# A hybrid attention layer on one Trainium2 core: the first gate's loads and sums given out among the first attention units

## The chip, the cores and the metric

The kernel is one launch on one core of a Trainium2 chip. The metric is the device time in microseconds of that launch, as a median of several runs. The engines are named as in the profile: PE (TensorE, matmuls), PEld (its weight loads), DVE (VectorE), ACT (ScalarE), POOL (GpSimd) and SP (SyncE, which issues the DMAs here).

## The reference, cut to what matters

The layer works on 512 tokens of width 1024. A vector `c` is multiplied into six modulation vectors; the third of them, `gt1`, is the first gate, and it is used only after the attention's output projection.

```python
mod = c @ w_ada[l] + b_ada[l]
sh1, sc1, gt1, sh2, sc2, gt2 = jnp.split(mod, 6, axis=-1)
h = rms_norm(x, g_pre_mix[l]) * (1.0 + sc1[:, None]) + sh1[:, None]
proj = h @ w_in[l]
...
o_nsa = nsa_attention(...)   # compressed, selected and windowed branches, gated
o_dsa = dsa_attention(...)   # a top-k choice of keys from an index, then attention
o = jnp.concatenate([o_nsa, o_dsa], axis=-1) @ w_out[l]
x = x + gt1[:, None] * rms_norm(o, g_post_mix[l])
h = rms_norm(x, g_pre_ffn[l]) * (1.0 + sc2[:, None]) + sh2[:, None]
y = jnp.square(jax.nn.relu(h @ w_up[l])) @ w_down[l]
x = x + gt2[:, None] * rms_norm(y, g_post_ffn[l])
```

## The kernel before, in words

All matmuls that need precision are split: an operand is rounded on ACT (`L123`, "hi") and the rest is subtracted on DVE or POOL (`L124`, "lo"), and each product is three matmuls. The stages are:

- **First projection (about 20 to 82 us).** Modulation columns for the first norm, then the column chunks A and B of `w_in` for all four token tiles.
- **Chunks D, C and E (about 82 to 190 us).** `proj` (`L392`) makes 24 matmuls for each of four token tiles: `pj_D`, `pj_C`, `pj_E`. Beside them run the rotary products (`rope`, `L398`, on DVE and POOL), the stacking and transposing of heads (`stack`, `stack_T`), the compressed keys and values (`cmp_pack`, `cmp_mm`: tiles `kcp_k`, `kcp_v`, `hid_k`, `hid_v`), the index scores of the top-k (`index_step`, `L549`: matmul `ix`, relu `rl` on ACT, weighted sum `wk` on DVE) and the top-k itself (`topk_round`, `L565`: sixteen rounds of MAX8 and MATCH_REPLACE8 on DVE for each of three token tiles).
- **Attention units (about 158 to 360 us).** Twelve units (`UNITS`, `L51`): a kind of attention ("s", "w" or "d") and a token tile. Each unit makes score matmuls `s_*`, a masked maximum on DVE (`L876`), an exponential on ACT (`L877`), scalings on DVE, transposes `tp_*`, and the product `O*`. The output projection (`op`, `L1006`) and the next norm are mixed in.
- **MLP (about 385 to 720 us).** Matmuls `up` and `dn`, back to back.

The order of the first 360 us is written by hand. `PLAN` (`L41`) is a table that gives each group of steps a start and a length in slots. `place` (`L813`) spreads the steps of a group evenly: step q of n goes to start + (q + 0.5) / n * length, and the integer part is its slot. Slots 0 to 18 are emptied one by one by the loop at `L832`, beside the steps of chunks D and C. Slots 19 to 34 are emptied by the loop over the units (`run(la, lc, slot(n + 19))`, near `L1090`), mixed with that unit's steps. The tile framework's scheduler then reorders each engine's instructions within what the program's dependences allow.

The group of the change is `g1`, the first gate (`g1_steps`, `L731`, over `vec_steps`, `L704`). It has 23 steps: one that loads the norm weights and two bias rows (`bb`, 256 KB each, broadcast to all partitions, in two of six buffers of a pool named `m2`); two loads of `wv_g` (512 KB each, in two buffers); six empty steps; then eight groups of four matmuls (`vs_g`, `L718`) that add up one half of the vector, each of the first six followed by the load of the next piece into the buffer just read. After the fourth and after the eighth group `finish` adds the bias on DVE (`L743`), spreads the row over the partitions with one matmul (`gv_g`, `L745`) and multiplies with the norm weights on DVE (`L746`). While it is being summed a half holds one PSUM bank of the tag "S", of which there are four; `pj_*`, `ix`, `s_*`, `op` and others use the same four. The result is first read by `outp_steps` (`L1012`) in slot 25. The same `vec_steps` makes `a2` (slots 25 to 27) and `sh2` (slots 29 to 32) later, from tiles `wv_a` and `wv_sh`, through the same two load buffers.

Of the kernel before, what the change touches and what calls it, by code (L numbers as in the profile page):

```python
# [45 lines left out]
    x22=(32.6, 0.1), h22=(33.35, 1.68), x23=(33.6, 0.1), sD=(0, 0.48), cl=(0.2, 4.48), lC=(0.5, 0.1),  # L46
    sC=(3.7, 2.94), lE=(8.2, 0.1), sE=(8.3, 5.379), ix=(8.2, 5.88), cpe=(10, 0.1), ck1=(11.1, 1.077),
    cv1=(13.2, 0.784), ck2=(11.7, 2.8), ck3=(15, 2.8), cv2=(14.6, 0.98), cv3=(15.2, 1.05), tk1=(13, 6),
    g1=(6, 8),
)  # L50
UNITS = [("s", 0), ("w", 0), ("s", 1), ("w", 1), ("d", 0), ("d", 1),  # L51
         ("s", 2), ("w", 2), ("d", 2), ("s", 3), ("w", 3), ("d", 3)]
# [1147 lines left out]
```

## Time and profile before

| what | value |
|---|---|
| runs | 733.19 us median of 3 (732.59 to 735.87) |
| the profiled execution's own time | 734.76 us |
| its span, first to last instruction | 733.0 us |
| mean granted clock of PE | 0.966 |
| busy: PE, DVE, ACT, POOL | 690.3, 457.1, 332.1, 129.2 us |

The profile names an instruction by its line, its engine, and what it writes and reads, with buffer numbers left out (`pj_C<-uh_C,hh`). A busy matmul row counts the time until its modelled end, and rows overlap; so the distance from one start to the next says more than the length of one. `x8` in a row of `vs_g` is one group of four matmuls (each makes two instructions). In brackets stands how long the engine had been idle, and what ended that.

### The profile page before, as it was taken

The page shows a single profiled execution, that of the slowest core. Times are in us where ns is not written, and L with a number is a line of the kernel's source. Part 1 is how long each engine was busy: PE and PEld are TensorE (multiplying, and loading weights), DVE is VectorE, ACT ScalarE, POOL GpSimd, SP SyncE. Part 2 cuts the span into 40 slices and gives each one's busy share as a digit, 9 for nine tenths or more (in the row PEclk, how much of TensorE's full clock was granted, in tenths as well). Part 3 has the DMA queues.
Part 4 walks back from the last instruction along what each step waited for, and adds up shares of the span by engine and source line. Part 5 has one row for each costly group of instructions (what it writes and reads, how often), then busy time and mean ns, then how long its engine had stood idle before and what let it go on. Part 6 is the DMA issues. An engine that isn't in the chain of part 4 may idle for free.

```text
span 733.0 us, 9979 instructions
## 1 busy us (share of the span) xinstructions
PE 690.3 (94%) x3601; PEld 539.3 (74%) x3601; DVE 457.1 (62%) x978; ACT 332.1 (45%) x691; POOL 129.2 (18%) x196
## 2 busy tenths in 40 slices
PE   4998979899989999899999999999999999999995
PEld 2776967788755576465699888888888888788884
DVE  4444637979989978774685464654734445443547
ACT  5433783725778569554475313322331332323222
POOL 3000193544634144222020000000000000000003
PEclk9999998969889999999999999999999999999998
DMA  8996451450006571462122352533415133231202
GB/s 246 312 322 211 115 172 59 110 120 1 1 1 161 172 185 30 115 230 86 58 87 66 103 164 99 170 117 116 132 64 178 58 114 115 81 121 58 86 1 114
DMA packets 67612, 87.15 MB, mean 119 GB/s; under 512 B 3974, under 2 KB 38890, under 8 KB 67563
## 3 DMA queue, kind: packets, MB, share of 16 engines
q1 hardware_dynamic: 67562, 86.52, 39.0%
q8 instruction: 28, 0.46, 0.3%
q14 instruction: 22, 0.17, 0.1%
HBM read 84.40 MB, written 2.10 MB: 118 GB/s over the span
## 4 chain that ended last, share of the span: by engine, by line
PE 77%; DVE 9%; DMA 7%; ACT 3%; issue 2%; SPq 2%; POOL 1%; POOLq 0%; DVEq 0%; ACTq 0%
PE up L1113 22%; PE dn L1154 22%; PE op L1006 6%; PE O L905 4%; PE pj_E L323 2%; PE pA L323 2%; DMA wm<-in_w_ada_dram 2%; PE pj_D L323 2%; PE pj_C L323 2%; PE pB L323 1%; SPq L161 1%; PE tp_w L899 1%; PE hid_v L622 1%; DVE m L567 1%; DMA rwA<-in_w_in_dram 1%
## 5 line engine op out<-in xcount | busy, mean ns | idle before, releaser
L1113 PE MATMUL up<-hh,uh_U 128*128 128x512 f32 (+1 forms) x288 | 104.6, 366 | 0.6 <-ACT hh L123 0.6
L1113 PE MATMUL up<-hh,ul_U 128*128 128x512 f32 (+1 forms) x288 | 104.9, 366 | 0.0
L1113 PE MATMUL up<-hl,uh_U 128*128 128x512 f32 (+1 forms) x288 | 104.0, 366 | 0.0
L1154 PE MATMUL dn<-uh_D,al 128*128 128x512 f32 x256 | 99.6, 389 | 0.0
L1154 PE MATMUL dn<-uh_D,ah 128*128 128x512 f32 x256 | 98.7, 391 | 0.0
L1154 PE MATMUL dn<-ul_D,ah 128*128 128x512 f32 x256 | 98.5, 389 | 0.0
L124 DVE TENSOR_TENSOR ul_D<-rw_D,uh_D 128x1024 fp32r<-128x1024 f32 (+1 forms) x35 | 41.3, 1181 | 47.7 <-ACT uh_D L123 45.4
L1160 DVE TENSOR_TENSOR y<-dn,y 128x512 f32<-128x512 f32 x56 | 38.3, 689 | 49.5 <-PE dn L1154 49.4
L206 POOL TENSOR_SCALAR ms<-sy 128x1 f32<-128x1 f32 x4 | 3.6, 912 | 341.6 <-ACT fj L1133 341.6
L1113 PEld LDWEIGHTS up<-hh,uh_U 128*128 128x128 f32 x288 | 54.3, 188 | 9.6 <-ACT hh L123 0.9
L1117 ACT ACTIVATE rl<-up 128x512 f32<-128x512 f32 x32 | 19.1, 598 | 92.6 <-PE dn L1154 59.2
L1113 PEld LDWEIGHTS up<-hh,ul_U 128*128 128x128 f32 x288 | 54.3, 189 | 8.8
L1113 PEld LDWEIGHTS up<-hl,uh_U 128*128 128x128 f32 x288 | 53.7, 189 | 9.0 <-DVE hl L124 0.2
L123 ACT CAST uh_U<-rw_U 128x1024 fp32r<-128x1024 f32 x32 | 33.7, 1052 | 55.1 <-PE dn L1154 51.9
L123 ACT CAST uh_D<-rw_D 128x1024 fp32r<-128x1024 f32 (+1 forms) x36 | 36.2, 1010 | 46.2 <-PE up L1113 37.5
L1154 PEld LDWEIGHTS dn<-uh_D,al 128*128 128x128 f32 x256 | 48.1, 188 | 10.2 <-issue 0.2
L1154 PEld LDWEIGHTS dn<-uh_D,ah 128*128 128x128 f32 x256 | 48.1, 188 | 10.1 <-issue 0.2
L1154 PEld LDWEIGHTS dn<-ul_D,ah 128*128 128x128 f32 x256 | 48.1, 188 | 10.1
L124 DVE TENSOR_TENSOR ul_U<-rw_U,uh_U 128x1024 fp32r<-128x1024 f32 x32 | 39.1, 1222 | 11.6 <-ACT uh_U L123 10.7
L1118 DVE TENSOR_TENSOR rl<-rl 128x512 f32<-128x512 f32 x32 | 22.1, 690 | 34.8 <-ACT rl L1117 34.8
L123 ACT CAST ah<-rl 128x512 fp32r<-128x512 f32 x32 | 19.8, 620 | 29.3 <-DVE rl L1118 29.2
L124 DVE TENSOR_TENSOR al<-rl,ah 128x512 fp32r<-128x512 f32 x32 | 22.0, 689 | 11.0 <-ACT ah L123 11.0
(407 smaller groups left out, 1486.2 us busy)
## 6 DMA issues: line engine op xcount, KB each, us to landing
rw_U<-in_w_up_dram SPq DMA_DIRECT2D x32, 512.0 KB, 4.7
rw_D<-in_w_down_dram SPq DMA_DIRECT2D x32, 512.0 KB, 3.6
wm<-in_w_ada_dram SPq DMA_DIRECT2D x32, 256.0 KB, 6.3
wv_g<-in_w_ada_dram SPq DMA_DIRECT2D x8, 512.0 KB, 6.2
rwo_a<-in_w_out_dram SPq DMA_DIRECT2D x16, 256.0 KB, 4.5
wv_a<-in_w_ada_dram SPq DMA_DIRECT2D x8, 512.0 KB, 5.5
rwo_b<-in_w_out_dram SPq DMA_DIRECT2D x16, 256.0 KB, 4.1
wv_sh<-in_w_ada_dram SPq DMA_DIRECT2D x8, 512.0 KB, 4.4
```

The source lines that it names most:

```text
L123: A.copy(hi, src)
L124: eng.tensor_tensor(lo, src, hi.bitcast(F32), op=OP.subtract)
L161: mod_in[k].append(SY.dma_start(wt[hf][:, v], wa[:, hf * 4:hf * 4 + 4, v * D + k * P:v * D + (k + 1) * P]))
L323: PE.matmul(ps[:, :n], l[:, t, k, :], r[:, k % 2, :n], start=(k == 0 and i == 0), stop=(k == KT - 1 and i == 2))
L567: mx = V.max(m8, work[t])
L905: mm = [PE.matmul(O[j][g * 64:(g + 1) * 64, :], vn[kb][:, self.vsl[g]:self.vsl[g] + 64], pts[kb, g][0], start=(first and kb == 0), stop=(l ...
L1006: PE.matmul(stt["ps"], l[:, kk, :], r[:, kk % 2, :], start=(kk == 0 and i == 0), stop=(kk == 7 and i == 2))
L1113: PE.matmul(pv[:, t0:t1, :], l[:, k % 2, fs], r[:, t0:t1, k, :], start=(n == 0), stop=(n == 23))
L1117: A.activation(rl, ps, AF.Relu)
L1118: V.tensor_tensor(rl, rl, rl, op=OP.mult)
L1154: PE.matmul(ps, l[:, t * P:(t + 1) * P], r[:, f % 2, :], start=(n == 0), stop=(n == 11))
L1160: V.tensor_tensor(ya, ps, ya, op=OP.add)
```

## The change

One pair of numbers in `PLAN`: the 23 steps of `g1` start at slot 17 and take 6 slots, where they started at slot 6 and took 8.

```diff
 PLAN = dict(
...
     cv1=(13.2, 0.784), ck2=(11.7, 2.8), ck3=(15, 2.8), cv2=(14.6, 0.98), cv3=(15.2, 1.05), tk1=(13, 6),
-    g1=(6, 8),
+    g1=(17, 6),
 )
```

By the formula the first sum moves from slot 9.3 to slot 19.5, and the last step from slot 13.8 to slot 22.9. What the scheduler makes of that is shown at three places.

**PE, from the last matmul of `pj_C` for token tile 0 to the first for tile 1.** `skp_ks` are transposes of keys, `kcT` is the transpose for the compressed keys, `ix_1_2` and `ix_1_3` are index scores. Before:

```order
L323 MATMUL pj_C_0_1140<-uh_C3_1021,hl_1_177 128x512
L417 MATMUL skp_ks3_1047<-identr_109,sk_ks3_969 128x128 x2
L417 MATMUL skp_ks0_1095<-identr_109,sk_ks0_1000 128x128 x2
L486 MATMUL kcT_1043<-ident_104,pjB_2_710 128x128
L552 MATMUL ix_1_2_1178<-k1a_685,qi_0_884 128x256
L553 MATMUL ix_1_2_1178<-k2a_686,qi_0_884 128x256
L718 MATMUL vs_g10_1173<-wv_g12_1184,c_sb_67 32x256 x4
L417 MATMUL skp_ks1_1167<-identr_109,sk_ks1_1040 128x128 x2
L718 MATMUL vs_g10_1173<-wv_g13_1259,c_sb_67 32x256 x4
L552 MATMUL ix_1_3_1186<-k1a_685,qi_0_884 128x256
L553 MATMUL ix_1_3_1186<-k2a_686,qi_0_884 128x256
L323 MATMUL pj_C_1_1210<-uh_C0_950,hh_1_176 128x512
```

And with the change:

```order
L323 MATMUL pj_C_0_1130<-uh_C3_1015,hl_1_177 128x512
L486 MATMUL kcT_1033<-ident_104,pjB_2_710 128x128
L417 MATMUL skp_ks3_1037<-identr_109,sk_ks3_969 128x128 x2
L417 MATMUL skp_ks0_1085<-identr_109,sk_ks0_1000 128x128 x2
L552 MATMUL ix_1_3_1169<-k1a_685,qi_0_884 128x256
L553 MATMUL ix_1_3_1169<-k2a_686,qi_0_884 128x256
L417 MATMUL skp_ks1_1157<-identr_109,sk_ks1_1030 128x128 x2
L323 MATMUL pj_C_1_1193<-uh_C0_950,hh_1_176 128x512
```

The third and fourth group of sums are gone from here (the first two stood a few rows earlier, inside `pj_C_0`), and `ix_1_2` has taken their place inside `pj_C_0`. In the built program `pj_C_1` has the PSUM bank that `ix_1_0` had, before and after; the relu that empties that bank is on ACT.

**PE, around the hidden layer of the compressed values (`hid_v`).** Before:

```order
L718 MATMUL vs_g11_1407<-wv_g16_1427,c_sb_67 32x256 x4
L622 MATMUL hid_v_1550<-kcp_v_1485,w1_v0_888 128x62 x8
L622 MATMUL hid_v_1550<-kcp_v_1485,w1_v1_890 128x62 x2
L417 MATMUL skp_C00_1581<-identr_109,sk_C00_1451 128x128 x2
L718 MATMUL vs_g11_1407<-wv_g17_1467,c_sb_67 32x256 x4
L417 MATMUL skp_C00_1581<-identr_109,sk_C00_1451 128x128 x2
L417 MATMUL skp_C01_1587<-identr_109,sk_C01_1454 128x128 x4
L622 MATMUL hid_v_1550<-kcp_v_1485,w1_v1_890 128x62 x6
L745 MATMUL gv_g11_1505<-bb_1_1019,ones_111 128x512
L552 MATMUL ix_3_3_1508<-k1a_685,qi_2_983 128x512
L553 MATMUL ix_3_3_1508<-k2a_686,qi_2_983 128x512
L323 MATMUL pj_E_0_1725<-uh_E0_1121,hh_1_176 128x512
```

With the change, eleven matmuls of `pj_E` for tile 0 stand ahead of `hid_v` (the last two of them are shown), and no sum of the gate is near:

```order
L323 MATMUL pj_E_0_1671<-uh_E1_1234,hh_1_176 128x512
L323 MATMUL pj_E_0_1671<-ul_E1_1235,hh_1_176 128x512
L622 MATMUL hid_v_1486<-kcp_v_1429,w1_v0_888 128x62 x8
L417 MATMUL skp_C00_1517<-identr_109,sk_C00_1401 128x128 x4
L417 MATMUL skp_C01_1523<-identr_109,sk_C01_1404 128x128 x4
L622 MATMUL hid_v_1486<-kcp_v_1429,w1_v1_890 128x62 x8
L323 MATMUL pj_E_0_1671<-uh_E1_1234,hl_1_177 128x512
```

**PE, between `pj_E` for tile 1 and for tile 2, with the change.** `s_s0_5` and `s_s0_6` are scores of the first attention unit. `wv_g10` and `wv_g11` are the two pieces that are loaded early; `wv_g12` is loaded into the buffer of `wv_g10`, whose group stands 17 rows above `wv_g12`'s:

```order
L323 MATMUL pj_E_1_1721<-uh_E3_1413,hl_1_177 128x512
L718 MATMUL vs_g10_1733<-wv_g11_1628,c_sb_67 32x256 x3
L873 MATMUL s_s0_5_1764<-k1s_687,qC_0_1516 128x128
L874 MATMUL s_s0_5_1764<-k2s_688,qC_0_1516 128x128
L718 MATMUL vs_g10_1733<-wv_g11_1628,c_sb_67 32x256
L873 MATMUL s_s0_6_1774<-k1s_687,qC_0_1516 128x128
L874 MATMUL s_s0_6_1774<-k2s_688,qC_0_1516 128x128
L417 MATMUL skp_C11_1578<-identr_109,sk_C11_1471 128x128 x4
L417 MATMUL skp_C20_1594<-identr_109,sk_C20_1510 128x128 x4
L718 MATMUL vs_g10_1733<-wv_g12_1769,c_sb_67 32x256 x4
L323 MATMUL pj_E_2_1797<-uh_E0_1111,hh_1_176 128x512
```

These sums are new here. The fourth group stands after `pj_E` for tile 2, the other four and both `gv_g` among the scores of the units "w" 0, "s" 1 and "w" 1.

On SP the norm weights and the first two pieces of `wv_g` stay where they were, in the first 45 us. The other six, and both loads of `bb`, move from the place after the loads of `rw_E` to a place after the first four pairs of `rwo_a` loads, one after the other, and directly ahead of the first two loads of `wv_a`.

## Rows read from the trace of the kernel before

**Rows 1.** The page: its first line and the busy time of each engine.

```profile
span 733.0 us, 9979 instructions
...
PE 690.3 (94%) x3601; PEld 539.3 (74%) x3601; DVE 457.1 (62%) x978; ACT 332.1 (45%) x691; POOL 129.2 (18%) x196
```

**Rows 2.** The table by windows from 100 to 240 us. Columns: the window, its length, busy us (and number) of PE, PEld, DVE, ACT and POOL, the granted clock of PE, the DMA engines' busy share, GB/s.

```profile
100.00:110.00 10.00, 6.07 (x48) 3.57 (x46) 1.55 (x4) 7.51 (x21) 9.10 (x18) 0.84 0.82 255
110.00:120.00 10.00, 9.19 (x39) 6.74 (x36) 6.04 (x17) 2.65 (x8) 1.91 (x5) 0.65 0.34 107
...
130.00:140.00 10.00, 10.00 (x66) 7.57 (x65) 10.00 (x25) 7.94 (x16) 6.37 (x8) 1.00 0.05 19
140.00:150.00 10.00, 8.09 (x54) 6.60 (x52) 8.49 (x20) 3.24 (x9) 3.69 (x5) 0.72 1.09 262
150.00:160.00 10.00, 10.00 (x40) 7.94 (x37) 7.17 (x19) 2.29 (x5) 3.83 (x6) 0.60 0.58 141
160.00:180.00 20.00, 19.23 (x113) 15.96 (x112) 19.28 (x72) 9.76 (x32) 10.12 (x15) 1.00 0.00 1
180.00:200.00 20.00, 18.97 (x112) 15.48 (x112) 19.53 (x76) 13.82 (x48) 12.94 (x22) 0.89 0.00 1
...
230.00:240.00 10.00, 8.56 (x72) 4.63 (x71) 10.00 (x28) 6.84 (x18) 4.10 (x4) 1.00 0.81 236
```

**Rows 3.** The chain that ended last, from 101 to 126 us. Columns: start, us, what.

```profile
102.45 6.48 DMA wv_g<-in_w_ada_dram
...
113.09 7.45 PE pj_C L323 x24
```

**Rows 4.** The timeline of PE from 101 to 113.5 us. Columns: start, length, engine, line, operation, what it writes and reads, count, and the idle time before it with what ended it.

```profile
101.75 1.07 PE L718 MATMUL vs_g<-wv_g,c_sb 128*32 128x256 f32 x16
...
105.35 0.33 PE L486 MATMUL kcT<-ident,pjB 128*128 128x128 f32 x1 [0.88 <-POOL pjB L406]
105.43 0.36 PE L552 MATMUL ix<-k1a,qi 128*128 128x256 f32 x1
...
108.97 1.08 PE L718 MATMUL vs_g<-wv_g,c_sb 128*32 128x256 f32 x8 [3.06 <-DMA wv_g<-in_w_ada_dram]
...
112.29 0.58 PE L552 MATMUL ix<-k1a,qi 128*128 128x256 f32 x1 [0.81 <-DVE bb L743]
...
112.89 0.63 PE L323 MATMUL pj_C<-uh_C,hh 128*128 128x512 f32 x1
```

**Rows 5.** The timeline of ACT from 104 to 116 us, same columns.

```profile
104.21 0.59 ACT L528 COPY pjC<-pj_C 128x512 f32<-128x512 f32 x1 [1.70 <-PE pj_C L323]
...
107.19 1.50 ACT L609 COPY kcp_k<-kcT 64x256 f32<-64x256 f32 x4
...
109.04 0.38 ACT L555 ACTIVATE rl<-ix 128x256 f32<-128x256 f32 x1
...
114.63 0.30 ACT L410 CAST sk_kw<-pjD 128x128 fp32r<-128x128 f32 x1 [0.84 <-DVE wk L559]
```

**Rows 6.** The timeline of POOL from 101 to 106 us, same columns.

```profile
101.52 2.38 POOL L124 TENSOR_TENSOR ul_E<-rw_E,uh_E 128x1024 fp32r<-128x1024 f32 x1
```

**Rows 7.** What DVE waited for between 100 and 222 us. Columns: DVE's instruction, what released it, us in total, times, longest.

```profile
DVE bb L743 <- PE vs_g L718: 7.9, 2, 6.1
...
DVE peT L600 <- PE pep_k L598: 2.4, 1, 2.4
DVE hx L629 <- PE hid_v L622: 1.9, 1, 1.9
...
DVE g L746 <- PE gv_g L745: 0.6, 1, 0.6
...
DVE wk L557 <- ACT rl L555: 0.4, 1, 0.4
```

**Rows 8.** The timeline of DVE, from 104 to 123 us and from 122 to 165 us: the first two bias sums, the first round of the top-k, the two gate products, the first masked maximum of the attention.

```profile
111.55 0.69 DVE L743 SCALAR_TENSOR_TENSOR bb<-bb,vs_g 128x512 f32<-128x512 f32 x1 [6.11 <-PE vs_g L718]
...
115.52 0.41 DVE L567 MAX8 m<-wk 128x8 f32<-128x256 f32 x1
...
129.17 0.67 DVE L746 TENSOR_TENSOR g<-gv_g,g 128x512 f32<-128x512 f32 x1
...
150.29 0.69 DVE L743 SCALAR_TENSOR_TENSOR bb<-bb,vs_g 128x512 f32<-128x512 f32 x1 [1.80 <-PE vs_g L718]
...
160.59 0.27 DVE L876 CUSTOM_DVE_ANT_0 P_s<-s_s,mask 128x128 f32<-128x128 f32 x1
```

**Rows 9.** The timeline of PE from 136 to 157 us.

```profile
136.54 0.64 PE L718 MATMUL vs_g<-wv_g,c_sb 128*32 128x256 f32 x8
137.11 0.50 PE L552 MATMUL ix<-k1a,qi 128*128 128x512 f32 x1
...
142.96 0.64 PE L718 MATMUL vs_g<-wv_g,c_sb 128*32 128x256 f32 x8 [1.06 <-DMA wv_g<-in_w_ada_dram]
144.45 4.53 PE L622 MATMUL hid_v<-kcp_v,w_v 128*128 128x62 f32 x20 [0.85 <-DVE kcp_v L612]
...
156.20 0.63 PE L323 MATMUL pj_E<-uh_E,hh 128*128 128x512 f32 x1
```

**Rows 10.** The view of the tile `wv_g`: from the issue of a load to its landing.

```profile
DMA to landing us min/median/max: 4.5/6.2/8.2
```

**Rows 11.** What PE waited for between 76 and 260 us: the sums of the later vector `a2`, by the same code.

```profile
PE vs_a L718 <- DMA wv_a<-in_w_ada_dram: 1.3, 1, 1.3
```

## Prediction

> **What bounds the kernel now.** I read the page first, then the table by windows, then the chain, and last the timelines of PE, ACT and DVE where the first gate stands. PE is busy for 690.3 of 733.0 us [rows 1], and the MLP, the last half, has no gaps; a change of order can win only before it. The table by windows shows where [rows 2]: from 100 to 110 us PE has 6.07 us of work and DVE 1.55; from 100 to 120 and from 140 to 160 us the granted clock is 0.60 to 0.84, so that part of the time PE works at 1.2 instead of 2.4 GHz. From 160 us on DVE is the fullest engine (19.28 and 19.53 of 20 us). The chain says what ends last in the first gap: a load of `wv_g` for 6.48 us and, behind the sums, the bias sum and an index score, the 24 matmuls of `pj_C` that take 7.45 us [rows 3]. The gate is not needed until slot 25, far later.
>
> So the two stretches are weighed apart from what follows. In the stretches (100 to 160 us) PE stalls and DVE stalls behind it. In the first attention units (160 to 220 us) DVE is full, and what arrives there is paid mostly in full. What counts is when DVE reaches the first masked maximum of the attention, at 160.59 us before [rows 8].
>
> **Part 1: the gap at 102 to 113 us.** Before, PE waits 3.06 us for the third piece and 0.81 us for the bank that the bias sum empties, and `pj_C` for tile 1 starts at 112.89 [rows 4]. With those sums gone it does not start at once: it needs the bank of `ix_1_0`, and the relu that frees it comes late in ACT's queue. Before, that relu ran from 109.04 to 109.42, behind the copy of `pj_C` (from 104.21), six key copies and four copies of `kcp_k` (1.50 us) [rows 5]. Now `pj_C_0` ends 0.8 us sooner (1.07 us of sums leave, one index pair comes, 0.3 us as an estimate from the 0.36 us of one `ix`, whose matmuls overlap [rows 4]), and two of the four copies stand behind the relu (0.75 us). `kcT`, which held PE until 105.35, does not hold it now: a 2.38 us subtraction on POOL has moved behind what `kcT` waits for [rows 4, 6]. So the relu ends at about 107.9 and `pj_C_1` starts 5.0 us earlier. PE still idles for some four of the five us before, so I let the low clock stand. If it stayed at 2.4 GHz, PE would gain at most the 0.35 that a mean of 0.65 leaves out [rows 2] of the 7.45 us of `pj_C` [rows 3], 2.6 us; DVE, which decides, gets none of it.
>
> DVE gains less than PE. Its first top-k round began at 115.52 [rows 8]. After the relu ACT has a second relu, the two copies of `kcp_k`, three key copies, a cast, two relus and a cast (0.38 + 0.75 + 1.1 + 0.3 + 0.8 + 0.3 = 3.6 us; copies and relus at the relu's 0.38 each, casts at 0.30 [rows 5]). Then come POOL's selection and what belongs to it, 0.9 us as from the last cast at 114.63 to the round at 115.52 [rows 5, 8]: 107.9 + 3.6 + 0.9 = 112.4. That is **3.1 us** (the bias sum's 0.69 us is inside). Two later waits of DVE go as well, for `peT` (2.4) and for a relu (0.4) [rows 7], since PE is five us early there and DVE three: **2.8 us**.
>
> **Part 2: 128 to 160 us.** Three more DVE instructions leave, 0.67 + 0.69 + about 0.68 us [rows 8]: **2.0 us**. Three waits leave: 1.8 us for the eighth group (the rest of the 7.9 us is part 1's 6.1), 1.9 for `hid_v`, 0.6 for the second spreading [rows 7]: **4.3 us**. `hid_v` was late because PE waited 1.06 us for the seventh piece and 0.85 us for `kcp_v`, and then did its 20 rows in 4.53 us at the low clock, until `pj_E` began at 156.20 [rows 2, 9]. Now eleven matmuls of `pj_E` cover the wait for `kcp_v`. I find PE some 5 us ahead of DVE at the first masked maximum, so DVE decides. Sum so far: 3.1 + 2.8 + 2.0 + 4.3 = **12.2 us**, DVE at about 148.4.
>
> **Part 3: what arrives at 150 to 205 us.** DVE gets its four instructions back: 0.69 + 0.69 + 0.67 + 0.68 = **2.7 us**, in full. PE gets eight groups and two spreadings. A group takes 0.57 us from start to start (136.54 to 137.11 [rows 9]), a spreading 0.50, as the index matmul of the same 128x512 in those rows: 4.6 + 1.0 = 5.6 us. PE has slack (19.23 and 18.97 of 20 us busy [rows 2], and the 5 us lead), but four PSUM banks limit how far it runs ahead, and one of them is now held by the sums. Between 0 and 5.6 I take **2.0 us**. The third piece can be loaded only when the first group has been read; a load takes 4.5 to 8.2 us to land [rows 10], and between the two groups stand some 3 us of PE work by the order. So PE waits 1.5 to 3 us there, and perhaps again at the seventh piece; less what DVE's own work covers I take **1.0 us** (bounds 0 and 6.1, twice the 3.06 of [rows 4]). Two of six `m2` buffers are held by `bb` here; two rotary products of `pj_E` now share one buffer, and a third takes `bb`'s first after the spreading: **0.5 us** (0 to 2). SP pays nothing: its queue is empty of other needs there (DMA share 0.00 to 0.01 [rows 2]), and the first loads of `wv_a`, now behind `wv_g`, still come some slots ahead of their use. The start of the kernel is unchanged, for the first two pieces stay there. After 220 us all waits are relative to what came before, so the lead is carried to the end.
>
> **Sum:** 12.2 - 2.7 - 2.0 - 1.0 - 0.5 = **6.0 us** less. The profiled execution took 734.76 us, so 728.8; it lies 1.6 us above the median of 733.19, and in terms of that median I predict **727.2 us**.
>
> One rule I weigh against this. Rows first: a wait for one piece (3.06 us, and 0.88 just before) was followed by a clock that fell from 1.00 to the low level and a mean of 0.65 over 110 to 120 us [rows 2, 4]; yet the same kind of sums for `a2`, which waited 1.3 us for a load, ran in a window with a clock of 1.00 [rows 2, 11]. The Trainium skill, "TensorE: Matmul & The Clock Gate", section "HAM oscillation — how this bites in real kernels", tells of a kernel whose short bursts of matmuls each wait for a DMA, and whose every burst then runs cold. By that rule the moved groups would bring the low clock along. The first case above agrees with it, the second does not.
>
> **Rivals.**
> - *The stall moves along (slower).* Six pieces are still loaded into two buffers. If PE stops at the third and again at the seventh as at 105 us, and works at 1.2 GHz after each, each place costs a wait of 3.06 us [rows 4] and the 3.5 us that a mean clock of 0.65 takes from ten [rows 2], 6.6 us, twice 13.1. With all of PE's 5.6 and DVE's 2.7 us paid: 12.2 - 8.3 - 13.1 = 9.2 us slower, **742.4 us**. It decides against the change once waits and clock there cost over 3.9 us. For it: the load's 4.5 us against 3 us of cover. Against it: `a2` [rows 2, 11], and that PE leads here. Chance 0.10.
> - *Nothing left (same).* DVE's top-k ends last from 122 us on, so only the part 1 gain of 3.1 + 2.8 us and 2 us of part 2 hold (the waits for `hid_v` and the groups are replaced by waits for PE's `pj_E`), and part 3 is paid with 2.7 + 5.6 us: 7.9 - 8.3 = 0.4 us slower, **733.6 us**. For it: DVE has 10.00 of 10 us in 130 to 140 [rows 2]. Against it: from 140 to 160 DVE idles for 4.3 us, and behind PE alone. Chance 0.23.
> - *All of it (faster still).* The attention units hide PE's part in DVE's shadow: 12.2 - 2.7 = 9.5 us, **723.7 us**. Chance 0.19.
> - That the change does not do what it says is excluded for six of the eight pieces by the order.
>
> **How the numbers follow.** My forecast has 0.48; its own gain reaches from 2.4 us (all of PE's 5.6 paid instead of 2.0) to 8.5 us (PE's part and the buffers' at nothing). A measurement of this kernel can tell about 0.5%, 3.7 us, from no change, and of the forecast's 0.48 I put 0.05 below that. Faster by more: 0.43 + 0.19 = 0.62; within: 0.05 + 0.23 = 0.28; slower by more: 0.10. The range reaches from 721.0, the whole 12.2 us with nothing paid back, to 734.6, nothing left and the wait for a piece (1.0 us) on top; beyond it lie the slower case and a little of the others.
>
> **What would show it.** Right: `pj_C_1` starts near 108 us instead of 112.89, DVE's first MAX8 near 112.4, `hid_v` at the full clock, the first masked maximum near 148, `vs_g` groups at 150 to 205 us with a wait of some 1 to 3 us for the third piece, DVE at 19 or more of 20 us there. Wrong: a clock of 0.5 to 0.7 behind the sums at 155 to 175 us, or DVE idle for several us at the first masked maximum.

## The result and the profile after

The changed kernel takes **729.98 us** (median of 6 runs, 728.45 to 732.34), the kernel before 733.26 us beside it (6 runs). The ratio is 0.9942, 95% interval 0.9918 to 0.9967. It is faster, by 3.3 us in the medians and 4.3 us by the ratio, where 6.0 us (727.2 us) had been forecast. Two more comparisons later gave 0.9971 [0.9949, 0.9993] and 0.9946 [0.9925, 0.9967], so 2 to 4 us is what the change is worth. The profiled execution took 730.62 us with a span of 728.9. One execution of the later run with sixteen fillers, the profiled one, ran at a mean clock of 0.56 from end to end (1133 us); it is in no ratio, and no row of its profile is used.

The page, first line and busy time; it answers to [rows 1]. PE is busy for 4.1 us less, DVE for 0.9 us more:

```profile
span 728.9 us, 9985 instructions
...
PE 686.2 (94%) x3601; PEld 535.1 (73%) x3601; DVE 458.0 (63%) x978; ACT 331.8 (46%) x691; POOL 128.9 (18%) x196
```

The table by windows, columns as in [rows 2]:

```profile
100.00:110.00 10.00, 6.89 (x37) 5.27 (x36) 3.65 (x7) 9.09 (x26) 10.00 (x20) 0.96 0.37 105
110.00:120.00 10.00, 10.00 (x42) 8.17 (x41) 8.31 (x27) 4.30 (x13) 4.73 (x10) 0.87 0.01 2
...
140.00:150.00 10.00, 5.83 (x40) 5.17 (x38) 10.00 (x26) 2.53 (x7) 9.18 (x13) 1.00 0.22 53
150.00:160.00 10.00, 9.44 (x50) 6.86 (x50) 8.70 (x35) 4.08 (x15) 1.84 (x3) 0.83 0.13 40
160.00:180.00 20.00, 19.54 (x118) 14.98 (x113) 17.46 (x68) 9.61 (x30) 8.28 (x14) 0.91 0.37 112
180.00:200.00 20.00, 19.08 (x148) 13.59 (x147) 18.80 (x70) 15.40 (x48) 11.62 (x20) 1.00 0.33 107
200.00:220.00 20.00, 19.45 (x117) 12.72 (x115) 20.00 (x84) 19.02 (x61) 5.55 (x7) 1.00 0.13 27
220.00:230.00 10.00, 6.96 (x45) 4.28 (x45) 10.00 (x25) 6.91 (x17) 5.32 (x3) 0.93 0.47 135
230.00:240.00 10.00, 10.00 (x51) 5.30 (x52) 7.63 (x22) 5.89 (x13) 1.65 (x2) 0.73 1.05 247
```

The reader sees three things. The clock from 100 to 120 us is 0.96 and 0.87 instead of 0.84 and 0.65. From 140 to 150 us DVE is full (10.00) and PE half idle (5.83) at a clock of 1.00; before, PE had 8.09 us there at a clock of 0.72 and DVE 8.49. And from 220 to 240 us PE idles, and then the clock is 0.73, where the kernel before had 1.00; that kernel had its own low clock (0.85) from 200 to 220 us, where the change has 1.00 throughout. The kernel before:

```profile
200.00:220.00 20.00, 17.06 (x99) 11.00 (x99) 17.48 (x81) 16.26 (x53) 5.76 (x10) 0.85 0.01 1
220.00:230.00 10.00, 8.93 (x48) 6.25 (x46) 10.00 (x32) 9.11 (x24) 5.19 (x3) 1.00 0.44 100
```

One sign that the prediction had named is missing: DVE was to be at 19 or more of 20 us behind 160 us, and it has 17.46 and 18.80, while PE has 19.54 and 19.08.

PE's timeline at the places that the prediction named; it answers to [rows 4] and [rows 9]:

```profile
104.29 0.33 PE L486 MATMUL kcT<-ident,pjB 128*128 128x128 f32 x1 [0.23 <-POOL pjB L406]
...
108.47 0.50 PE L323 MATMUL pj_C<-uh_C,hh 128*128 128x512 f32 x1 [2.14 <-ACT rl L555]
...
137.73 1.99 PE L622 MATMUL hid_v<-kcp_v,w_v 128*128 128x62 f32 x16
...
150.56 0.80 PE L323 MATMUL pj_E<-uh_E,hh 128*128 128x512 f32 x1 [4.73 <-DVE mx L876]
151.15 0.63 PE L323 MATMUL pj_E<-ul_E,hh 128*128 128x512 f32 x1
151.58 0.63 PE L323 MATMUL pj_E<-uh_E,hl 128*128 128x512 f32 x1
...
156.82 0.64 PE L718 MATMUL vs_g<-wv_g,c_sb 128*32 128x256 f32 x8
...
162.16 0.64 PE L718 MATMUL vs_g<-wv_g,c_sb 128*32 128x256 f32 x8
...
199.34 1.06 PE L745 MATMUL gv_g<-bb,ones 128*128 128x512 f32 x2
200.23 0.63 PE L899 MATMUL tp_s<-ident,P_s 128*128 128x128 f32 x4
...
228.41 1.79 PE L922 MATMUL sc<-kcx,qC 128*128 128x64 f32 x8 [1.71 <-DVE mx L876]
```

`pj_C` for tile 1 starts at 108.47 (near 108 was forecast), behind the relu, as the prediction said. `hid_v` runs at the full clock, 16 rows in 1.99 us where 20 had taken 4.53. The third piece's group (162.16) waits for nothing. PE stands 4.73 us from 145.83 on because it is that far ahead of DVE, and the spacing of `pj_E` soon behind it is 0.43 us (151.15 to 151.58). The second long stop, 1.71 us for a masked maximum, ends at 228.41.

DVE's timeline, with the first round of the top-k and the first masked maximum; it answers to [rows 8]:

```profile
112.92 0.43 DVE L567 MAX8 m<-wk 128x8 f32<-128x256 f32 x1 [0.40 <-POOL wk L562]
...
125.54 0.70 DVE L559 SCALAR_TENSOR_TENSOR wk<-rl,wi,wk 128x384 f32<-128x384 f32 x1
...
126.84 2.46 DVE L559 SCALAR_TENSOR_TENSOR wk<-rl,wi,wk 128x384 f32<-128x384 f32 x1
...
150.23 0.27 DVE L876 CUSTOM_DVE_ANT_0 P_s<-s_s,mask 128x128 f32<-128x128 f32 x1
```

The first round comes at 112.92 (112.4 forecast), the first masked maximum at 150.23 (148.4 forecast), 10.4 us sooner than before. In between one weighted sum takes 2.46 us where its like takes 0.70; more on that at the end.

### The profile page after: what moved, and what is told of

Its sections match the earlier page's. It is cut to its first block, busy times and chain, and to the rows that moved or that the text cites. A ratio compares the mean times of both kernels' runs of the same rounds, so it can differ in the third digit from the quotient of the medians.

```text
span 728.9 us, 9985 instructions
## 1 busy us (share of the span) xinstructions
PE 686.2 (94%) x3601; PEld 535.1 (73%) x3601; DVE 458.0 (63%) x978; ACT 331.8 (46%) x691; POOL 128.9 (18%) x196
## 4 chain that ended last, share of the span: by engine, by line
PE 74%; DVE 12%; DMA 4%; POOL 3%; issue 2%; ACT 2%; SPq 2%; POOLq 0%; DVEq 0%; ACTq 0%
PE up L1113 23%; PE dn L1154 22%; PE op L1006 6%; PE O L905 3%; PE pj_E L323 3%; PE pA L323 2%; DMA wm<-in_w_ada_dram 2%; PE pj_C L323 2%; DVE wk L570 1%; PE pB L323 1%; DVE m L567 1%; SPq L161 1%; PE tp_d L899 1%; DVE P_d L894 1%; DMA rwA<-in_w_in_dram 1%
```

## The experiments

The theory: the lead of DVE at the first masked maximum (12.2 us forecast) is carried to the end, less what the gate costs where it arrives, 6.2 us, of which DVE's four instructions are the largest part. The first rival: the arrival costs little, and the lead is lost later for other reasons. The second: PE's sums are the cost.

Profiled executions start chunk D (the first matmul of `pj_D`) at 79.0 to 83.3 us, ahead of the moved work (only the run without any sums leaves out two loads before it). So leads over the kernel before are given from there, as the time of an event in the kernel before (160.59 us for the first masked maximum [rows 8]) less that in the kernel of the row, with the same difference at chunk D's start taken off. "Ratio" is that of the timed runs to the kernel before, beside it on the chip.

`P_d<-s_d,wk` is the masked maximum of a unit "d" that uses the top-k, at 216.88 us in the kernel before; `dn` is the last stage.

| kernel | first masked maximum | first `P_d<-s_d,wk` | last `dn` | ratio [95%] |
|---|---|---|---|---|
| the change | 11.2 | 8.5 | 4.9 | 0.9942 [0.9918, 0.9967] |
| the change again | 11.3 | 6.6 | 2.6 | 0.9971 [0.9949, 0.9993] |
| the change beside the fillers | 10.6 | 6.0 | 1.8 | 0.9946 [0.9925, 0.9967] |
| no sums | 9.5 | 13.7 | 13.2 | 0.9811 [0.9786, 0.9837] |
| two loads, old place | 3.8 | 6.1 | 3.2 | 0.9924 [0.9894, 0.9954] |
| second half late | 5.8 | 5.8 | 1.4 | 0.9920 [0.9890, 0.9951] |
| start 20 | 9.4 | 8.0 | 7.3 | 0.9888 [0.9863, 0.9913] |
| no DVE part | 11.5 | 5.6 | 0.7 | 0.9957 [0.9935, 0.9978] |
| few sums | 12.8 | 12.4 | 7.3 | 0.9866 [0.9837, 0.9896] |
| start 21 | 11.2 | 8.0 | 6.2 | 0.9926 [0.9901, 0.9952] |
| ten fillers | 11.1 | 6.6 | 2.5 | 0.9962 [0.9943, 0.9981] |
| start 19 | 9.9 | 4.6 | 3.6 | 0.9917 [0.9886, 0.9948] |

One profile is one execution: the three of the change differ by 2.5 us in the third column and by 3.1 us in the fourth, and the fourth differs from the timed ratio by up to 4.5 us (second half late). Verdicts go by the ratios, and the columns say where. Chunk D starts at 81.9 to 82.5 us in the three profiles of the change, at 79.0 in few sums and at 80.5 to 80.6 in start 20 and no sums; whether the timed runs have these differences of 1 to 3 us too is not known, and if so, they are in the ratios.

**No sums at all.**

```diff
-        return [begin] + vec_steps(c0, "g1", finish)
+        return [begin] + [none] * 22
```

(and `begin` without the two loads of `bb`.)

> Leaves out the gate's matrix product: its eight loads, the two bias loads, all its sums, both spreadings and DVE's four instructions; the gate is the norm weights alone. So the first gap has what the change has, and nothing arrives in the first attention units. My theory (what arrives at 150 to 205 us is paid with 2.7 us on DVE and 3.5 us on PE, 6.2 in all): some 4 to 7 us under the changed kernel, 723 to 726 us. Rival (the arrival costs little, and the lead of some 10 us at 214 us is lost after it, between 216 and 266 us, where PE and DVE are full in turn): 728 to 730 us, with a lead over the kernel before that shrinks after 216 us here too.

Measured: 0.9811, 721.82 us against 735.71. The table by windows from 160 us on:

```profile
160.00:180.00 20.00, 18.91 (x108) 15.83 (x106) 19.09 (x69) 9.54 (x27) 10.94 (x19) 0.91 0.00 1
180.00:200.00 20.00, 16.39 (x114) 12.29 (x114) 19.86 (x90) 18.94 (x64) 10.29 (x17) 1.00 0.01 2
200.00:220.00 20.00, 18.57 (x115) 11.59 (x112) 20.00 (x73) 19.01 (x55) 7.51 (x8) 1.00 0.32 79
220.00:240.00 20.00, 19.63 (x134) 12.14 (x134) 19.15 (x49) 11.90 (x27) 4.63 (x4) 1.00 0.66 192
```

The rival's first half falls: the arrival is dear. Without it the lead grows from 9.5 to 13.7 us before 209 us, and only 0.5 of it is lost after that; the clock from 180 to 220 us is 1.00 (before 0.89 and 0.85), though it is 0.91 from 160 to 180 us, where it was 1.00. Between 0.9811 and the change's three ratios (mean 0.9953) lie 1.4%, some **10 us** (8.3 to 11.4 by the last column): that is the price of the arrival, where 6.2 had been forecast. The rival's second half, a loss for other reasons, does not fall with it: see the next run.

**Two loads, in the old place.** Pieces 2 to 7 read the first two pieces again.

```diff
         def load(i):
+            if nm == "g1" and i > 1:
+                stt[i] = stt[i % 2]
+                return
```

> The kernel before, with six of the gate's eight loads left out: the sums of pieces 2 to 7 read the first two pieces again. Sums and DVE's instructions stay where they were. Theory (the sums' places cost through the waits for loads, 3.06 and 1.06 us, and the low clock behind them): pj_C for tile 1 starts near 109 us, clock 1.00 at 145 to 155 us, a gain of 2 to 5 us, 728 to 731 us. Rival (the bank behind the relu and DVE's own instructions set the time, the loads don't): 732 to 734 us, with the clock as low as before.

Measured: 0.9924. The first gap behaves as the theory has it (`pj_C` for tile 1 at 109.24). The second does not:

```profile
141.77 4.10 PE L622 MATMUL hid_v<-kcp_v,w_v 128*128 128x62 f32 x18 [2.37 <-DVE kcp_v L612]
```

The wait for `kcp_v` is 2.37 us now, and the clock from 140 to 150 us 0.52. So the theory's clock of 1.00 was missed: there the waits for loads were not the cause of the low clock. That the change cures it by the eleven matmuls of `pj_E` ahead of `hid_v` is read from the order; no run tests it apart. The lead at the first masked maximum is 3.8 us, a third of the change's. Yet the timed ratio is no worse than the change's: taking the loads' waits away in the old place was worth about as much at the end as the whole move. Nothing arrives late here, and still the lead falls from 6.1 to 3.2 us behind 209 us. So a loss there does not need an arrival.

**Only the second half late.**

```diff
-    g1=(6, 8),
+    g1=(6, 8 * 16 / 23), g1b=(17 + 6 * 16 / 23, 6 * 7 / 23),
...
-        g1=g1s, a2=a2s
+        g1=g1s[:16], g1b=g1s[16:], a2=a2s
```

> Only the gate's second half (four groups, one spreading, two DVE instructions, pieces 6 and 7) goes to the late place; the first half with loads 2 to 5 stays between chunks D and C. Theory (the two stretches add up, 5.9 of 12.2 us from the first and 6.3 from the second, before the payment): about half the gain, 731 to 732 us, the first MAX8 at 115 to 116 us and the first masked maximum near 153 to 155. Rival A (only the first gap counts): 733 us. Rival B (DVE is the bound after 122 us and the first gap is made up anyway): all of the gain, 729 to 730 us.

Measured: 0.9920, and in the trace a lead of 5.8 us at the first masked maximum, half of 11.2, with 3.29 us of waiting for the third piece as before. So the two stretches do add up, as the theory had it; but the timed ratio is no worse than that of the whole change (rival B's number). That only half of the gate arrives late would fit it, by a price that grows with what arrives; it is not shown, for in the trace the loss behind 209 us is as large as in the change (5.8 to 1.4).

**Start 20.**

```diff
-    g1=(17, 6),
+    g1=(20, 5),
```

> The change with the gate's steps still later, start 20 and length 5 instead of 17 and 6: the sums stand in the units w 1, d 0 and d 1, and the last spreading right before the scores of unit s 2. Theory (the gate's matmuls then fill idle time of PE at 205 to 230 us, which the changed kernel has before its low clock at 228 to 235 us): 726 to 729 us, and no low clock there. Rival (DVE's instructions meet DVE at its fullest, and the output projection waits for the gate): 730 to 733 us.

Measured: 0.9888, 726.79 us, as the theory had it: faster than both kernels, with an interval that does not touch the three of the change. The table by windows:

```profile
190.00:200.00 10.00, 6.69 (x56) 4.11 (x54) 9.26 (x32) 7.15 (x21) 4.38 (x7) 1.00 0.68 211
200.00:220.00 20.00, 19.99 (x137) 12.54 (x136) 19.82 (x81) 19.34 (x58) 7.52 (x7) 1.00 0.50 154
220.00:240.00 20.00, 20.00 (x137) 12.44 (x136) 19.90 (x57) 13.03 (x32) 5.24 (x5) 1.00 0.79 194
```

PE does 19.99 and 20.00 of 20 us from 200 on (18.57 and 19.63 without the sums), at a clock of 1.00. There is no low clock from 190 us on. The arrival costs 0.77% here (0.9888 against 0.9811 beside it), 5.7 us, against 10 us at start 17; and from the first `P_d<-s_d,wk` on almost none of the lead is lost (8.0 to 7.3). It is the best of four starts and was measured once; its neighbours 19 and 21 give 0.9917 and 0.9926.

**The change again**, for comparison with the next three.

> The changed kernel as it is, for comparison on the same chip. 0.992 to 0.997 of the kernel before.

Measured: 0.9971 [0.9949, 0.9993], 732.03 us.

**No DVE part.** The bias sum and the product with the norm weights are left out; two copies of one column stay.

```diff
-            V.scalar_tensor_tensor(bb[half], bb[half], 0.25, ps, op0=OP.mult, op1=OP.add)
...
-            V.tensor_tensor(g, pg, g, op=OP.mult)
+            if half == 1:
+                V.tensor_copy(g[:, 0:1], pg[:, 0:1])
+                V.tensor_copy(g[:, 1:2], ps[:, 0:1])
```

> The changed kernel, in which DVE neither adds the bias nor multiplies with the norm weights: two copies of one column are left of its four instructions, so the sums, spreadings, loads and PSUM banks stay. Of the 10.1 us that the arrival costs (the last matmul ends 14.2 us earlier than before without the sums, 4.1 us with them), theory A (DVE is full from 160 to 230 us, its 2.7 us come back about one to one): 2 to 4 us under the changed kernel. Rival B (PE's sums in the first units, 5.6 us at full price, and what they push are most of it): under 1.5 us.

Measured: 0.9957 against 0.9971 beside it, 1 us, within the intervals (which leave room for some 3 us); the mean of the change's three ratios, 0.9953, lies on the other side, and the lead at the last `dn` is 0.7 us, no better than in the change. What PE waited for from 180 to 236 us (columns: instruction, releaser, us in total, times, longest):

```profile
PE sc L923 <- DVE mx L877: 2.3, 1, 2.3
PE s_s L874 <- DVE mx L877: 2.0, 1, 2.0
```

So PE's long stops for a masked maximum are there without DVE's part of the gate too.

Theory A has nothing for it: leaving out 2.7 us of DVE's work wins next to nothing, though DVE was the fullest engine there before. The trace says why. These are the same stretch, from the first masked maximum to the first `P_d<-s_d,wk`, in the kernel before, in the change and without DVE's part (columns as in [rows 2]):

```profile
160.59:216.88 56.29, 51.73 (x300) 40.19 (x299) 52.57 (x211) 36.72 (x122) 27.74 (x44) 0.91 0.01 1
150.23:209.17 58.94, 57.22 (x367) 41.20 (x368) 53.90 (x217) 37.74 (x124) 23.31 (x39) 0.94 0.26 81
148.31:210.45 62.14, 58.41 (x358) 40.91 (x358) 53.32 (x214) 36.72 (x120) 23.36 (x39) 0.91 0.24 77
```

and what DVE waited for most in the change (150 to 209 us) and without DVE's part (148 to 210.5 us):

```profile
DVE P_s L876 <- PE s_s L874: 2.4, 4, 1.0
DVE P_w L876 <- PE s_w L874: 0.8, 1, 0.8
...
DVE P_s L877 <- PE s_s L875: 3.0, 4, 1.7
DVE P_w L877 <- PE s_w L875: 2.6, 3, 1.7
```

With the sums in it, PE is the fuller engine (57.22 of 58.94 us), and DVE is idle for 5.0 us, mostly waiting for PE's scores (in the two other profiles of the change for 7.1 us). Without its part of the gate DVE is idle for 8.8.

**Few sums.** Four matmuls in place of 32, the rest as in the change.

```diff
+            if nm == "g1":
+                if q == 1:
+                    PE.matmul(stt["ps"][:, n * 256:n * 256 + 256], c_sb[:, 0:1].to_broadcast([P, P]), stt[i][:, 0, :],
+                              start=True, stop=True)
-            for j in range(4):
+            for j in range(0 if nm == "g1" else 4):
```

> The changed kernel with 4 matmuls in place of the 32 of the gate's sums; loads, spreadings, banks and DVE's four instructions stay. Theory A (DVE's share is the main one): 0 to 2 us under the changed kernel. Rival B (PE's 5.6 us are paid in full): 4 to 7 us under it.

Measured: 0.9866 against 0.9971 beside it, 1.05%, **7.7 us** (by the intervals some 3 us less or more): rival B. Against the mean of the change's three ratios it is 6.4 us. In the trace the lead is 12.4 us at the first `P_d<-s_d,wk`, near the 13.7 without any sums, against 8.5, 6.6 and 6.0 in the change: 3.9 to 6.4 us. 28 matmuls of the gate take 4.0 us by the spacing of 0.57 us for four [rows 9], so they are paid in full, and perhaps more than that. (With them go PE's reads of four of the eight pieces; as no sum waited for a piece in the change, that should matter little.) Behind 209 us the lead falls by 5.1 us all the same, to 7.3, though the clock there is 1.00 from 210 to 270 us. So that loss is not made by the sums.

**Start 21.**

```diff
-    g1=(17, 6),
+    g1=(21, 4),
```

> The gate's steps at start 21, length 4, a step beyond the start of 20 that gave 0.989. Theory (idle time of PE at 205 to 230 us takes the sums for nothing): 0.985 to 0.990 of the kernel before. Rival (the fourth and the last group come so late that the output projection waits for the gate, which is read in slot 25, and loads crowd the wv_a loads): 0.990 to 0.998.

Measured: 0.9926 [0.9901, 0.9952], the rival's range: later than start 20 is not better.

**Ten fillers.** Matmuls of no use that keep PE at work ahead of the wait that ends at 228.41.

```diff
+            if nm == "a2" and i == 1:
+                for _ in range(10):
+                    PE.matmul(stt["ps"][:, 256:384], ident, ident, start=True, stop=True)
             if i % 4 == 3:
                 finish(half, stt["ps"])
```

> The changed kernel with ten matmuls of no use (128x128, into columns of the bank of vs_a that are overwritten later), of which five stand right ahead of the score matmuls sc that wait 1.71 us for DVE at 226.7 us, in the changed kernel before the clock falls to 0.5 for some 7 us (228 to 235 us, clock 0.57 in both windows of 4 us). Theory (this low clock costs half of 7 us): the clock stays at 1.00 there, 1.5 to 3.5 us under the changed kernel run beside it. Rival (DVE sets the time there and PE's clock does not count): the same or up to 2 us slower.

> The changed kernel as it is, beside the others: 0.992 to 0.998 of the kernel before, the clock low behind the wait for sc.

Measured: 0.9962 [0.9943, 0.9981], and the change beside it 0.9946 [0.9925, 0.9967]. The table by windows with the fillers:

```profile
220.00:228.00 8.00, 6.67 (x49) 4.01 (x48) 8.00 (x17) 5.71 (x13) 5.33 (x3) 1.00 0.41 108
228.00:236.00 8.00, 7.74 (x59) 4.63 (x57) 8.00 (x27) 3.93 (x9) 1.66 (x2) 1.00 0.96 249
```

and that of the change for the second of them:

```profile
228.00:236.00 8.00, 7.59 (x38) 4.31 (x38) 6.46 (x21) 3.52 (x9) 1.34 (x2) 0.57 0.94 233
```

The clock stays at 1.00, as intended, instead of 0.57 (0.67 and 0.79 in the two other profiles of the change), and the time does not fall: the rival holds. In the traces the lead goes from 6.6 to 2.5 us, as in the change again without fillers (6.6 to 2.6). DVE, busy for 6.46 to 7.85 of 8 us in the profiles of the change, is now full with 8.00. The fillers take some 2.2 us of PE themselves, so a gain of that size from the clock alone is not excluded.

**Sixteen fillers.** The same edit with `range(16)`.

> The same with sixteen such matmuls, eleven of them behind the last scores of unit s 2 and ahead of sc. Theory: clock 1.00 at 228 to 236 us, 1 to 3 us under the changed kernel. Rival: 1 to 4 us slower than it, by the matmuls' own time.

Measured: 0.9938 [0.9911, 0.9965], not to be told from the change beside it.

**Start 19.**

```diff
-    g1=(17, 6),
+    g1=(19, 6),
```

> Start 19 and length 6: the sums from slot 21.5 on, so more room between the loads than with start 20 and length 5 (0.989), where PE waited 0.51 and 0.96 us for pieces. Theory (PE's idle time from 205 us on takes the sums, and the waits for pieces go): 0.986 to 0.990. Rival (the place in the order decides, by which waits of PE for DVE fall long): anything from 0.988 to 0.997.

Measured: 0.9917 [0.9886, 0.9948], inside the rival's range; PE waited 1.28 us for a piece at 192.03, so the extra room between the loads did not end that wait. The clock is 1.00 over 185 to 190 us and 0.74 over 190 to 195.

## Why the prediction was right, and where its sum was off

**The way it goes and the range: right.** 729.98 us lies between 721.0 and 734.6, and the gain is clear of the measurement's uncertainty. But the range is wide: it also holds what the rivals "nothing left" (733.6) and "all of it" (723.7) gave, so the time alone does not tell them apart. That the sum came within 2 to 4 us is in part luck: the price was too low by some 4 us, and its parts were the wrong way round.

**Part 1: right.** `pj_C` for tile 1 at 108.47 behind the relu, the first round at 112.92 (2.6 us sooner, 3.4 from chunk D's start; 3.1 forecast). The clock recovers there, on which the prediction had not counted.

**Part 2: right.** `hid_v` at the full clock, and PE 4.73 us ahead of DVE at the first masked maximum, where "some 5 us" had been found. The lead there is 10.4 us (11.2 from chunk D's start) against 12.2. Half the gate moved gives half of it. The weighted sum of 2.46 us stands in this stretch; that its 1.8 us over the usual 0.70 explain the missing 1.0 is read from the trace and not tested.

**Part 3: the step that failed.** It was put as 2.7 us on DVE "in full", 2.0 of 5.6 on PE, 1.0 for a load, 0.5 for buffers. The runs show some 10 us in all: DVE's share about 1 us as measured (no DVE part), that of 28 of PE's 32 sums 7.7 us by the times and 3.9 to 6.4 us in the traces up to 209 us (few sums). The two were weighed the wrong way round. The rows had shown DVE fuller than PE over 40 us, but by little, 38.81 against 38.20 us [rows 2], and "fullest" was taken over to the kernel after. With more than 5 us put on PE and 2.7 on DVE, PE is the fuller one: in the change PE is busy for 57.22 of 58.94 us there and DVE is idle for 5.0, mostly waiting for scores, some of which stand behind the sums in PE's order. So PE's work is paid in full and DVE's is not. A spreading also costs PE more than 0.5: `gv_g` is two instructions, and the next start comes 0.89 us behind it (199.34 to 200.23). The load wait was priced too high: it is 0 us in the change, since the third piece landed in the 4.7 us between the end of the first group, which frees its buffer (156.82 + 0.64), and its own group at 162.16; loads took 3.5 to 6.1 us here, against 4.5 to 8.2 [rows 10]. The buffers' 0.5 us was not tested apart.

**"The lead is carried to the end": not in the change.** Of the lead at the first `P_d<-s_d,wk` the change loses 3.6 to 4.2 us by the end, in all three profiles. The sum had put this at nothing, and it is the other part of the 10 us. It is not the arrival as such: no sums loses 0.5, but the starts 19, 20 and 21 lose only 1.0, 0.7 and 1.8 with the whole gate arriving, while few sums loses 5.1, no DVE part 4.9, and two loads 2.9 with nothing arriving late. Nor does it hang on the low clock at 228 to 235 us: with the fillers that is gone and 4.1 us are lost. Why the order at start 17 loses it and that at start 20 does not is open: the scheduler changes the order of all three engines from one start to the next, and no run here held the order fixed.

**The clock rule.** The moved groups did not bring the low clock along: the windows from 160 to 200 us have 0.91 and 1.00, and so they have without any sums. The Trainium skill, "TensorE: Matmul & The Clock Gate", section "HAM oscillation — how this bites in real kernels", has bursts that each wait for a DMA; in the change no moved group waited for one, so it does not test this. Three other starts have such waits, and they do not agree: with 1.28 us that end at 192.03 in start 19 the clock is 0.74 over 190 to 195 us (1.00 over the five us before), while with 0.51 and 0.96 us in start 20 it is 1.00 over 190 to 200 us, and with 1.00 us at 200.31 in start 21 it is 1.00 over 200 to 210 us.

## What to carry to other kernels

When work is moved into a stretch in which two engines are nearly full, add it to each of them before asking which one decides: the engine that was fullest before need not be it after. Here 28 small matmuls cost PE at least their own 4.0 us, and 2.7 us of DVE's work next to nothing, because DVE then waited for PE. Bound such a price by a run that leaves the work out altogether; it gives about the most that a placement can win (14 us here), and a few other starts then cost little to try (start 20 gives 8 us instead of 3, in one comparison). Do not take a lead in the middle of the kernel for a gain at its end: here up to 5 us of it went for reasons that stayed open. And lifting a low clock won nothing measurable in the one place where it was tried.

## What the runs showed of the hardware

In seven profiles (the change three times, no sums, no DVE part, few sums, start 20), one DVE instruction of two tensor inputs that falls beside POOL's second subtraction `ul_E` takes 2.34 to 2.63 us instead of 0.4 to 0.7. POOL's timeline in the change:

```profile
126.47 2.41 POOL L124 TENSOR_TENSOR ul_E<-rw_E,uh_E 128x1024 fp32r<-128x1024 f32 x1 [0.64 <-ACT uh_E L123]
```

The weighted sum started at 126.84 and ended at 129.30, after POOL's 128.88. In the kernel before, the same subtraction ran at 133.92 for 2.57 us, and what DVE began beside it (MAX8 and replacing, one tensor input) kept its time:

```profile
135.39 0.54 DVE L570 MATCH_REPLACE8 wk<-m,wk 128x384 f32<-128x384 f32 x1
135.85 0.41 DVE L567 MAX8 m<-wk 128x8 f32<-128x256 f32 x1
```

The Trainium skill, "SBUF — State Buffer", section "SBUF: two separate sides", says that DVE and GpSimd lock a port pair against each other for a whole instruction when DVE reads two inputs from SBUF. The trace agrees: 0.70 us became 2.46 us. A change of order can thus cost 1.8 us without any wait that the profile names.
